# Fixing the order of high and low matmuls in the last gate tiles and in the output projection of a hybrid diffusion layer

## The chip, the cores and the metric

The kernel runs on one core of a Trainium2 chip. Its time is the device time of one launch in microseconds (us), taken without a profiler; the profile is one further execution. Each time below is from the runs of the kernel before, from its profile, or worked out from them as told.

## The reference

One transformer layer over 256 latent tokens and 256 context tokens of width 2048, in float32. Cut to the stages that this text speaks of:

```python
h_l = modulate(rms_norm(x, norm1_w), sh1, sc1)
# ... gated linear attention -> ya, differential attention -> yb
g_a, g_b = jnp.split(jax.nn.sigmoid(h @ w_gate + b_gate), 2, axis=-1)
mix = (g_a * (ya @ w_proj_gla) + g_b * (yb @ w_proj_diff)) @ w_out
x_new = x + g1 * mix
h2_l = modulate(rms_norm(x_new, norm2_w), sh2, sc2)
x_new = x_new + g2 * conv_ffn(h2_l, w_up, conv_w, conv_b, w_down)
```

`w_gate` is 2048 x 4096, `w_out` 2048 x 2048, `w_up` 2048 x 11264, `w_down` 5632 x 2048. A conditioning vector, multiplied by `w_ada`, gives the shifts, scales and gates (`sh1` to `g2`).

## The kernel before

**Halves.** TensorE works on float32 data that ScalarE and VectorE split in two: a rounded high half and the low half that is left. An activation block `A[k]` (128 channels by 256 tokens) holds both halves side by side, low first. A weight block of 512 columns (four 128 x 128 matrices, called a quad here) comes in by DMA as `wraw`; ScalarE copies it to `whi` (L206), and VectorE subtracts that to get `wlo` (L213); each of the two has four buffers in turn. For each 128 x 128 matrix there is a pair of matmuls: the high one (L262) multiplies `whi` with both halves of `A[k]`, 512 columns; the low one (L264) multiplies `wlo` with the high half of `A[k]`, 256 columns. A tile of 128 outputs is 16 pairs, or four quads, written by `col_tile`.

**Orders of a quad.** `col_tile` has three written orders: `TURN` is h0 l0 h1 l1 h2 l2 h3 l3 (h: high, l: low); `ENDED` ends in l2 l3 h3; `SHIFTED` is h0 h1 l0 h2 l1 h3 l2 l3, which draws the high halves one step ahead. Without a list of orders a tile has `TURN` three times and then `ENDED`, and this order only says in which order the program is written: a scheduler that simulates time while it builds places each engine's instructions, and it may take the high half of the next quad, or a matmul of another tile, ahead of a low half. With a list the tile is tied: each of its matmuls is held behind the one before it in the list, in one chain through all tied tiles (`chain`).

**Stages.** They follow one another on TensorE: a sweep over the first projections, the two attentions, 32 gate tiles (`gate_tile`, the last of them after the attention has ended), the two branch projections (`pga`, `pgb`), 16 output projection tiles (`mix`), six up tiles that are worked in an inner loop over k on activations that are not yet normalized (`up`, L1178 to L1180, inputs `raw0` to `raw15`), 82 up tiles by `col_tile` (`upg`, `upv`), and 16 down tiles of 11 quads each (`down`). The up tiles and the down tiles are tied already; their list puts `SHIFTED` at quads 0, 4, 7, 11, ... of nine (three for down) tiles and `ENDED` at the last of these.

**Between output projection and up tiles.** Each output projection tile is added to `x` (L1144, L1145), squared (L1150) and, from the ninth on, scaled to `raw` for the six unnormalized up tiles (L1124, L1125). The second sum of squares (`ss`, L1158) is a matmul of TensorE; from it ScalarE and VectorE make the root, and then normalize the 16 blocks one by one: `h2t` (L1166, VectorE), high half (L1167, ScalarE), low half (L1168, VectorE). The last of these blocks, k = 15, is called `a_1450` in the rows, the one before `a_1380`. Each engine works its queue strictly in the order in which the scheduler left it. The first upg tile reads block k with its k-th pair, so that its 16th pair needs `a_1450` whole.

```python
TURN = "h0 l0 h1 l1 h2 l2 h3 l3".split()
ENDED = "h0 l0 h1 l1 h2 l2 l3 h3".split()
SHIFTED = "h0 h1 l0 h2 l1 h3 l2 l3".split()
```

Of the kernel before, what the change touches and what calls it, by code (L numbers as in the profile page):

```python
# [146 lines left out]
def layer_kernel(tc, I, out):  # L147
# [3 lines left out]
    with es:  # L151
# [26 lines left out]
        def after(later, earlier):  # L178

            tc.add_manual_dep(later.ins, earlier.ins.name,  # L180
                              mybir.DependencyInfo(mybir.DependencyClass.NoSync, mybir.DependencyReason.DATA),
                              reason="activation table order")
# [14 lines left out]
        def flush(work=later):  # L197
            for step in [work.pop(0) for _ in range(len(work))]:
                step()

        def split(raw, n, lows=None):


            hi = st.tile([P, 512], F32R, tag="hi", bufs=4, name="whi")
            lo = st.tile([P, 512], F32R, tag="lo", bufs=4, name="wlo")
            copied[0] = S.copy(hi[:, :n], raw)  # L206
            if pin[0]:
                tc.keep_in_program_order(copied[0])
            splits[0] += 1
            e = G if splits[1] and splits[0] % splits[1] == 0 else V  # L210

            def low():
                i = e.tensor_tensor(lo[:, :n], raw, hi[:, :n].bitcast(F32), op=ALU.subtract)  # L213
                if pin[0]:
                    tc.keep_in_program_order(i)
                if e is V:
                    copied[1] = i

            if lows is None:
                low()  # L220
            else:
                lows.append(low)
            return hi, lo

        def fetch(src, n):
            raw = st.tile([P, 1024], F32, tag="raw", bufs=4, name="wraw")
            nc.sync.dma_start(raw[:, :n], src)
            return raw
# [5 lines left out]
        TURN = "h0 l0 h1 l1 h2 l2 h3 l3".split()  # L234
        ENDED = "h0 l0 h1 l1 h2 l2 l3 h3".split()
        SHIFTED = "h0 h1 l0 h2 l1 h3 l2 l3".split()

        def col_tile(src, acts, b, orders=None):

            nk = src.shape[1]
            nq = nk // 4
            tied = orders is not None
            orders = orders or [TURN] * (nq - 1) + [ENDED]
            for k0 in range(0, nk, 8):
                kn = min(8, nk - k0)
                if k0:  # L250
                    flush()
                raw = fetch(src[:, k0:k0 + kn, :].rearrange("p a b -> p (a b)"), kn * P)
                for kk in range(0, kn, 4):
                    whi, wlo = split(raw[:, kk * P:(kk + 4) * P], 4 * P)
                    order = orders[(k0 + kk) // 4]
                    for which in order:
                        j = int(which[1])
                        k = k0 + kk + j
                        sl = slice(j * P, (j + 1) * P)
                        first, last = k == 0 and which == "h0", k >= nk - 4 and which == order[-1]  # L260
                        if which[0] == "h":
                            i = PE.matmul(b.rearrange("p (a b) -> p a b", a=2), whi[:, sl], acts[k], start=first, stop=last)  # L262
                        else:
                            i = PE.matmul(b[:, T:], wlo[:, sl], acts[k][:, 1, :], start=False, stop=last)  # L264
                        if tied:
                            if chain:
                                after(i, chain[0])
                            chain[:] = [i]
                    if k0 and not kk:
                        flush(latest)  # L270
# [32 lines left out]
        A, B, C = [], [], []  # L303
# [350 lines left out]
        def ada_next(n):  # L654

            ada_due[0] += n
            while ada_at[0] < min(128, int(ada_due[0])):
                if len(ada_raw) == ada_pool[1]:
                    ada_dot()
                ada_load()  # L660
# [273 lines left out]
        with tc.tile_pool(name="diff", bufs=1) as pd:  # L934
# [96 lines left out]
            gates, ya, yb = {}, {}, {}  # L1031

            def gate_tile(j):
                ada_next(GATE_ADA[len(gates)])
                b = acc_bank("gate")
                col_tile(I["w_gate"][j], A, b)
                if j == len(C):
                    C.append(hp.tile([P, 2, T], F32, tag=f"c{j}", name=f"C{j}"))
                gates[j] = C[j % KT][:, j // KT, :]
                S.activation(gates[j], b[:, :T], AF.Identity, bias=vcol("b_gate", j))  # L1040
                V.tensor_tensor(gates[j], b[:, T:], gates[j], op=ALU.add)
# [6 lines left out]
            order = [j for k in range(KT) for j in (k, KT + k)]  # L1048
# [41 lines left out]
        for c in range(KT):  # L1090
# [7 lines left out]
            for b, j in ((ba, c), (bb, 16 + c)):  # L1098
                t = p3.tile([P, T], F32, tag="pt", bufs=2, name="pt")
                i = added(t, b)  # L1100
# [29 lines left out]
        for c in range(KT):  # L1130
            b = acc_bank("mix")
            if 0 < c < half:
                ada_next(1)
            col_tile(I["w_out"][c], A, b)
            if c == half:
                ada_done(16)
                ada_done(32)
                V.tensor_scalar(a2, adav[:, 32:48], 1.0, None, op0=ALU.add)
                V.tensor_tensor(a2, a2, vcol("norm2", 0, 16), op=ALU.mult)
                V.tensor_scalar(a2, a2, -0.5 / D, None, op0=ALU.mult)  # L1140
            xr = p3.tile([P, T], F32, tag="xr", bufs=2, name="xr")
            nc.scalar.dma_start(xr, I["xl"][:, c, :])
            x1.append(C[c][:, 0, :])
            V.scalar_tensor_tensor(xr, b[:, :T], adav[:, c:c + 1], xr, op0=ALU.mult, op1=ALU.add)  # L1144
            i = V.scalar_tensor_tensor(x1[c], b[:, T:], adav[:, c:c + 1], xr, op0=ALU.mult, op1=ALU.add)  # L1145
            if c >= half:
                for k in range(2 * (c - half), 2 * (c - half) + 2):
                    unnormed(k, i, summed)
            sq = p3.tile([P, T], F32, tag="sq2" if c else "sq_sum", bufs=2 if c else 1, name="sq2")
            S.activation(sq, x1[c], AF.Square)  # L1150
            if c == 0:
                sq_sum = sq
            elif c < KT - 1:
                summed = G.tensor_tensor(sq_sum, sq_sum, sq, op=ALU.add)
# [43 lines left out]
        with tc.tile_pool(name="ffn", bufs=1) as pf:  # L1198
# [25 lines left out]
                split_act(g[:, 1, :], g[:, 0, :], ug)  # L1224
                gs.append(g)

            def orders(n, nq, first, last):


                shifted = [i for j in range(0, nq * (last - first + 1) - 3, 7) for i in (first * nq + j, first * nq + j + 4)]  # L1230
                q = range(n * nq, (n + 1) * nq)
                return [ENDED if i == (last + 1) * nq - 1 else SHIFTED if i in shifted else TURN for i in q]

            for j in range(UPS // 2):
                gated(j, ups[2 * j], ups[2 * j + 1])
            for j in range(UPS // 2, FT):
# [11 lines left out]
            for c in range(KT):  # L1248
                b = acc_bank("down")
# [21 lines left out]
```

## Time and profile before

| what | us |
|---|---|
| time, median of three runs | 1700.16 |
| lowest, highest | 1699.24, 1700.27 |
| time of the profiled execution | 1700.9 |
| its span, first to last instruction | 1699.1 |
| TensorE busy in the span | 1680.0 |

The profiled execution took 0.7 us more than the median, and 1.8 us of its time lie outside the span. The granted clock is a mean of 0.999 of full speed. A matmul's duration covers its pipeline, so that neighbours overlap: what a matmul costs is the distance from its start to the next start, and not its duration.

### The profile page before, as it was taken

What the parts mean: (1) busy time and instruction counts of PE and PEld (TensorE: products, weight loads), DVE (VectorE), ACT (ScalarE), POOL (GpSimd) and SP (SyncE); (2) the same over time, 40 slices, a digit from 0 to 9 for tenths busy, and PEclk for the clock granted to TensorE, in tenths of its full rate; (3) what the DMA queues carried; (4) which work ended last, traced back from release to release, by engine and by line L of the source; (5) the groups of instructions that cost most, each with busy time, mean ns of one, the idle gap of its engine ahead of it and who ended that gap; (6) DMA issues with size and microseconds to landing.
All of it is one profiled execution on the core that took longest, in us unless ns stands there. A gap on an engine that the chain in (4) does not pass through costs nothing.

```text
span 1699.1 us, 29122 instructions
## 1 busy us (share of the span) xinstructions
PE 1680.0 (99%) x10460; PEld 1461.7 (86%) x10460; DVE 1241.0 (73%) x2375; ACT 980.0 (58%) x1984; POOL 310.9 (18%) x331
## 2 busy tenths in 40 slices
PE   7999999999999999999999999999999999999999
PEld 5779999998787888888888998888888888888887
DVE  5556765867688888788988797787878787644443
ACT  5324554756355777666766686666666666444443
POOL 0000213131210000001323200222222222222222
PEclk9999999999999999999999999999999999999999
DMA  9995532434566555688777566676767676666664
GB/s 384 402 408 194 165 127 90 140 109 155 181 200 233 172 188 186 203 280 279 267 260 261 181 200 217 217 238 224 237 227 237 222 241 223 199 203 193 199 201 135
DMA packets 108451, 368.75 MB, mean 217 GB/s; under 512 B 12176, under 2 KB 17040, under 8 KB 108304
## 3 DMA queue, kind: packets, MB, share of 16 engines
q1 hardware_dynamic: 103264, 362.51, 64.0%
q10 hardware_dynamic: 5040, 4.37, 0.8%
q8 instruction: 82, 1.34, 0.3%
q14 instruction: 65, 0.53, 0.1%
HBM read 364.73 MB, written 2.10 MB: 216 GB/s over the span
## 4 chain that ended last, share of the span: by engine, by line
PE 91%; DMA 4%; DVE 3%; ACT 1%; issue 1%; POOL 0%; SPq 0%; DVEq 0%; ACTq 0%
PE down L262 9%; PE upg L262 9%; PE upv L262 9%; PE gate L262 7%; PE down L264 5%; PE upg L264 5%; PE sweep L350 5%; PE upv L264 4%; PE gate L264 4%; PE mix L262 4%; PE mix L264 2%; PE pgb L262 2%; PE ab L350 2%; PE pga L262 2%; DMA ada<-in_w_ad 2%; PE dk L313 2%
## 5 line engine op out<-in xcount | busy, mean ns | idle before, releaser
L206 ACT CAST whi<-wraw 128x512 fp32r<-128x512 f32 (+2 forms) x1004 | 606.5, 608 | 397.3 <-PE down L262 110.5
L213 DVE TENSOR_TENSOR wlo<-wraw,whi 128x512 fp32r<-128x512 f32 (+2 forms) x888 | 608.6, 694 | 251.9 <-ACT whi L206 242.1
L213 POOL TENSOR_TENSOR wlo<-wraw,whi 128x512 fp32r<-128x512 f32 x116 | 157.0, 1353 | 576.4 <-ACT whi L206 555.5
L262 PE MATMUL down<-g,whi 128*128 128x512 f32 x704 | 243.6, 392 | 0.0
L262 PE MATMUL upg<-a,whi 128*128 128x512 f32 x656 | 229.0, 391 | 0.0
L262 PE MATMUL upv<-a,whi 128*128 128x512 f32 x656 | 229.0, 391 | 0.0
L264 PE MATMUL down<-g,wlo 128*128 128x256 f32 x704 | 195.4, 280 | 0.7 <-DVE wlo L213 0.7
L264 PE MATMUL upv<-a,wlo 128*128 128x256 f32 x656 | 182.8, 280 | 0.0
L264 PE MATMUL upg<-a,wlo 128*128 128x256 f32 x656 | 182.6, 280 | 0.0
L262 PE MATMUL gate<-a,whi 128*128 128x512 f32 x512 | 180.5, 398 | 0.7 <-ACT whi L206 0.7
L338 DVE CUSTOM_DVE_ANT_0 araw<-araw,cb 128x1024 f32<-128x1024 f32 x128 | 159.5, 1248 | 11.4 <-DMA araw<-in_w_ada 11.3
L262 PEld LDWEIGHTS down<-g,whi 128*128 128x128 f32 x704 | 131.0, 187 | 28.3
L262 PEld LDWEIGHTS upv<-a,whi 128*128 128x128 f32 x656 | 122.4, 187 | 26.6
L262 PEld LDWEIGHTS upg<-a,whi 128*128 128x128 f32 x656 | 122.4, 187 | 26.5
L264 PE MATMUL gate<-a,wlo 128*128 128x256 f32 x512 | 140.4, 284 | 0.0
L264 PEld LDWEIGHTS down<-g,wlo 128*128 128x128 f32 x704 | 132.9, 189 | 1.9 <-DVE wlo L213 1.0
L264 PEld LDWEIGHTS upv<-a,wlo 128*128 128x128 f32 x656 | 123.9, 189 | 0.5
L264 PEld LDWEIGHTS upg<-a,wlo 128*128 128x128 f32 x656 | 123.9, 189 | 0.5
L262 PEld LDWEIGHTS gate<-a,whi 128*128 128x128 f32 x512 | 94.4, 188 | 20.5 <-ACT whi L206 1.0
L264 PEld LDWEIGHTS gate<-a,wlo 128*128 128x128 f32 x512 | 96.5, 189 | 6.2 <-issue 1.8
L262 PE MATMUL mix<-a,whi 128*128 128x512 f32 x256 | 88.8, 396 | 0.0
L264 PE MATMUL mix<-a,wlo 128*128 128x256 f32 x256 | 69.0, 280 | 0.0
(343 smaller groups left out, 3324.9 us busy)
## 6 DMA issues: line engine op xcount, KB each, us to landing
wraw<-in_w_up SPq DMA_DIRECT2D x164, 512.0 KB, 4.3
araw<-in_w_ada SPq DMA_DIRECT2D x128, 512.0 KB, 4.9
wraw<-in_w_down SPq DMA_DIRECT2D x80, 512.0 KB, 3.9
ada<-in_w_ad SPq DMA_DIRECT2D x64, 512.0 KB, 10.0
wraw<-in_w_gate SPq DMA_DIRECT2D x64, 512.0 KB, 4.3
wraw<-in_w_in SPq DMA_DIRECT2D x58, 512.0 KB, 4.2
wraw<-in_w_proj SPq DMA_DIRECT2D x32, 512.0 KB, 4.3
wraw<-in_w_out SPq DMA_DIRECT2D x32, 512.0 KB, 4.6
```

The lines of the kernel that those rows point to most:

```text
L206: copied[0] = S.copy(hi[:, :n], raw)
L213: i = e.tensor_tensor(lo[:, :n], raw, hi[:, :n].bitcast(F32), op=ALU.subtract)
L262: i = PE.matmul(b.rearrange("p (a b) -> p a b", a=2), whi[:, sl], acts[k], start=first, stop=last)
L264: i = PE.matmul(b[:, T:], wlo[:, sl], acts[k][:, 1, :], start=False, stop=last)
L313: PE.matmul(o, whi[:, sl], hi[k], start=first and j == 0, stop=False)
L338: i = V.tensor_tensor_reduce(raw, raw, cb[:, q * 1024:(q + 1) * 1024], 1.0, 0.0, op0=ALU.mult, op1=ALU.add, accum_out=ada2[:, j, q:q + 1])
L350: return kept(PE.matmul(*args, **kw))
```

## The change

The function that lists the orders moves out of the feed-forward stage to `col_tile`, and two more stages use it. `orders(n, nq, first, last)` gives the list for tile n of nq quads: `SHIFTED` at quads 0, 4, 7, 11, 14, 18, ... counted from tile `first`, `ENDED` at the last quad of tile `last`, `TURN` everywhere else. Gate tiles 24 to 31 get a list with `SHIFTED` in tiles 24 to 28; output projection tiles 3 to 15 get one with `SHIFTED` in tiles 3 to 8. What is computed, and the number of matmuls, stay the same.

```diff
+        def orders(n, nq, first, last):
+            shifted = [i for j in range(0, nq * (last - first + 1) - 3, 7) for i in (first * nq + j, first * nq + j + 4)]
+            q = range(n * nq, (n + 1) * nq)
+            return [ENDED if i == (last + 1) * nq - 1 else SHIFTED if i in shifted else TURN for i in q]
+
-        def col_tile(src, acts, b, orders=None):
+        def col_tile(src, acts, b, turns=None):
...
-            tied = orders is not None
-            orders = orders or [TURN] * (nq - 1) + [ENDED]
+            tied = turns is not None
+            turns = turns or [TURN] * (nq - 1) + [ENDED]
...
-                    order = orders[(k0 + kk) // 4]
+                    order = turns[(k0 + kk) // 4]
...
                 b = acc_bank("gate")
-                col_tile(I["w_gate"][j], A, b)
+                n = len(gates)
+                col_tile(I["w_gate"][j], A, b, orders(n, 4, 24, 28) if n > 23 else None)
...
-            col_tile(I["w_out"][c], A, b)
+            col_tile(I["w_out"][c], A, b, orders(c, 4, 3, 8) if c > 2 else None)
```

The queues of the two kernels as they are built show what the scheduler makes of this. In the changed kernel line numbers after 235 are 7 to 8 higher. GpSimd's and SyncE's queues stay as they were.

TensorE where gate tile 23 passes to tile 24, before (`a_219`, `a_330`, `a_402`, `a_481` are blocks 0 to 3, `a_1450` block 15):

```order
L264 MATMUL gate<-a_1450,wlo 128x256
L262 MATMUL gate<-a_1450,whi 128x512
L262 MATMUL gate<-a_219,whi 128x512
L264 MATMUL gate<-a_219,wlo 128x256
L262 MATMUL gate<-a_330,whi 128x512
L264 MATMUL gate<-a_330,wlo 128x256
L262 MATMUL gate<-a_402,whi 128x512
L264 MATMUL gate<-a_402,wlo 128x256
L262 MATMUL gate<-a_481,whi 128x512
L264 MATMUL gate<-a_481,wlo 128x256
```

The same place in the changed kernel:

```order
L271 MATMUL gate<-a_1450,wlo 128x256
L269 MATMUL gate<-a_1450,whi 128x512
L269 MATMUL gate<-a_219,whi 128x512
L269 MATMUL gate<-a_330,whi 128x512
L271 MATMUL gate<-a_219,wlo 128x256
L269 MATMUL gate<-a_402,whi 128x512
L271 MATMUL gate<-a_330,wlo 128x256
L269 MATMUL gate<-a_481,whi 128x512
L271 MATMUL gate<-a_402,wlo 128x256
L271 MATMUL gate<-a_481,wlo 128x256
```

The high half of block 1 moved ahead of the low half of block 0, and so on to the end of the quad.

TensorE in the six unnormalized up tiles, before, from the last use of the first `raw` block (`raw_10507`) by the tile `up_11012` to the second use of the third block (`raw_10577`) by that tile:

```order
L1179 MATMUL up_11012<-raw_10507,whi 128x258
L1180 MATMUL up_11012<-raw_10507,wlo 128x258
L1178 MATMUL up_11012<-raw_10512,whi 128x258
L1179 MATMUL up_11012<-raw_10512,whi 128x258
L1180 MATMUL up_11012<-raw_10512,wlo 128x258
L1179 MATMUL up_11011<-raw_10577,whi 128x258
L1180 MATMUL up_11011<-raw_10577,wlo 128x258
L1158 MATMUL ss_11043<-sq_11007,ones 128x256
L1178 MATMUL up_11012<-raw_10577,whi 128x258
L1179 MATMUL up_11012<-raw_10577,whi 128x258
```

The same in the changed kernel:

```order
L1187 MATMUL up_11012<-raw_10507,whi 128x258
L1188 MATMUL up_11012<-raw_10507,wlo 128x258
L1186 MATMUL up_11012<-raw_10512,whi 128x258
L1187 MATMUL up_11012<-raw_10512,whi 128x258
L1188 MATMUL up_11012<-raw_10512,wlo 128x258
L1186 MATMUL up_11012<-raw_10577,whi 128x258
L1187 MATMUL up_11012<-raw_10577,whi 128x258
```

The two matmuls on `up_11011` went earlier, and the second sum of squares (`ss`, row L1158 before) went nine matmuls later, so that only four matmuls are left between the last use of one high half and the first use of the one that takes its buffer.

ScalarE at the first upg tile, before: the copies are `whi` of that tile's four quads and of the next tile, `shift` and `C_...` belong to the six up tiles' convolutions:

```order
L206 CAST whi<-wraw 128x512 x3
L1190 COPY shift<-up_11009 128x1
L1190 COPY shift<-up_11010 128x1
L1190 COPY shift<-up_11011 128x1
L1167 ACTIVATE a_1380<-h2t,adav 128x256
L1190 COPY shift<-up_11012 128x1
L1190 COPY shift<-up_11013 128x1
L1190 COPY shift<-up_11014 128x1
L1167 ACTIVATE a_1450<-h2t,adav 128x256
L206 CAST whi<-wraw 128x512
```

The same in the changed kernel, from the high half of `a_1380` to that of `a_1450`:

```order
L1175 ACTIVATE a_1380<-h2t,adav 128x256
L206 CAST whi<-wraw 128x512
L1200 ACTIVATE C_8721<-C_8721,shift 128x256
L1200 ACTIVATE C_8604<-C_8604,shift 128x256
L1219 ACTIVATE C_6289<-C_8721,vec 128x256
L1200 ACTIVATE C_8487<-C_8487,shift 128x256
L206 CAST whi<-wraw 128x512
L1219 ACTIVATE C_6569<-C_8604,vec 128x256
L1200 ACTIVATE C_8370<-C_8370,shift 128x256
L1219 ACTIVATE C_6846<-C_8487,vec 128x256
L206 CAST whi<-wraw 128x512
L1175 ACTIVATE a_1450<-h2t,adav 128x256
```

Three copies for the next tile (its quads 0, 1 and 2) and seven convolution steps now stand ahead of `a_1450`; before it was the fourth instruction after `a_1380`.

VectorE at the same place, before:

```order
L1168 SCALAR_TENSOR_TENSOR a_1380<-h2t,adav,a_1380 128x256
L1191 TENSOR_TENSOR C_8370<-up_11012,n2y 128x256
L1191 TENSOR_TENSOR C_8253<-up_11013,n2y 128x256
L1191 TENSOR_TENSOR C_8074<-up_11014,n2y 128x256
L1168 SCALAR_TENSOR_TENSOR a_1450<-h2t,adav,a_1450 128x256
L213 TENSOR_TENSOR wlo<-wraw,whi 128x512
L1212 SCALAR_TENSOR_TENSOR C_6289<-C_8721,vec,C_6289 128x255
```

The same in the changed kernel:

```order
L1176 SCALAR_TENSOR_TENSOR a_1380<-h2t,adav,a_1380 128x256
L213 TENSOR_TENSOR wlo<-wraw,whi 128x512
L1220 SCALAR_TENSOR_TENSOR C_6289<-C_8721,vec,C_6289 128x255
L213 TENSOR_TENSOR wlo<-wraw,whi 128x512
L1220 SCALAR_TENSOR_TENSOR C_6569<-C_8604,vec,C_6569 128x255
L1220 SCALAR_TENSOR_TENSOR C_6846<-C_8487,vec,C_6846 128x255
L1222 SCALAR_TENSOR_TENSOR C_6289<-C_8721,vec,C_6289 128x255
L213 TENSOR_TENSOR wlo<-wraw,whi 128x512
L1176 SCALAR_TENSOR_TENSOR a_1450<-h2t,adav,a_1450 128x256
```

The low half of `a_1450` now stands behind three splits for the next tile and four convolution steps.

## Rows read from the trace of the kernel before

**Rows 1.** The page: busy time of the engines, and shares of the chain of work that ended last.
```profile
PE 1680.0 (99%) x10460; PEld 1461.7 (86%) x10460; DVE 1241.0 (73%) x2375; ACT 980.0 (58%) x1984; POOL 310.9 (18%) x331
...
PE 91%; DMA 4%; DVE 3%; ACT 1%; issue 1%; POOL 0%; SPq 0%; DVEq 0%; ACTq 0%
```

**Rows 2.** The chain of work that ended last, in order of time, in the gate stage: start, us, what. Each row is the two low halves that end a tile, l2 l3 of `ENDED`; of tiles 24 and 31.
```profile
739.95 0.24 PE gate L264 x2
...
779.52 0.24 PE gate L264 x2
```

**Rows 3.** The timeline of TensorE, tied up tiles in plain `TURN`: the first high half of tile 19 and of tile 81 (start, us, operation, tiles and shape, count).
```profile
1100.52 0.39 PE L262 MATMUL upv<-a,whi 128*128 128x512 f32 x1
...
1444.41 0.39 PE L262 MATMUL upv<-a,whi 128*128 128x512 f32 x1
```

**Rows 4.** The same view, tied up tiles with `SHIFTED`: the first high halves of tile 8 (two in a row, the first `SHIFTED` quad) and of tile 18.
```profile
1039.24 0.63 PE L262 MATMUL upg<-a,whi 128*128 128x512 f32 x2
...
1094.97 0.39 PE L262 MATMUL upg<-a,whi 128*128 128x512 f32 x1
```

**Rows 5.** The chain that ended last in the output projection: the two low halves in a row of tiles 2, 9, 10 and 14, and in tile 10 the one low half for which TensorE waited. In tiles 2 to 9 the two low halves are followed by the tile's last high half; in tiles 10 to 14 they are the tile's last matmuls.
```profile
885.79 0.24 PE mix L264 x2
...
925.36 0.24 PE mix L264 x2
...
928.89 0.30 PE mix L264
...
931.42 0.24 PE mix L264 x2
...
953.71 0.24 PE mix L264 x2
```

**Rows 6.** The timeline of TensorE at the first upg tile: its first high half, the high halves of blocks 14 and 15, and the first of the upv tile.
```profile
994.50 0.40 PE L262 MATMUL upg<-a,whi 128*128 128x512 f32 x1
...
999.72 0.39 PE L262 MATMUL upg<-a,whi 128*128 128x512 f32 x1
...
1000.07 0.39 PE L262 MATMUL upg<-a,whi 128*128 128x512 f32 x1
...
1000.41 0.39 PE L262 MATMUL upv<-a,whi 128*128 128x512 f32 x1
```

**Rows 7.** The timeline of ScalarE there; in brackets the engine's idle time before the row and what ended it.
```profile
995.57 0.56 ACT L1167 ACTIVATE a<-h2t,adav 128x256 fp32r<-128x256 f32 x1
996.38 0.62 ACT L206 CAST whi<-wraw 128x512 fp32r<-128x512 f32 x1 [0.26 <-ACT a L1167]
...
998.21 0.49 ACT L1192 ACTIVATE C<-C,shift 128x256 f32<-128x256 f32 x1
998.61 0.60 ACT L206 CAST whi<-wraw 128x512 fp32r<-128x512 f32 x1
999.12 1.09 ACT L1211 ACTIVATE C<-C,vec 128x256 f32<-128x256 f32 x2
1000.12 0.49 ACT L1192 ACTIVATE C<-C,shift 128x256 f32<-128x256 f32 x1
1000.52 0.60 ACT L206 CAST whi<-wraw 128x512 fp32r<-128x512 f32 x1
```

**Rows 8.** The timeline of VectorE there.
```profile
998.35 0.47 DVE L1168 SCALAR_TENSOR_TENSOR a<-h2t,adav,a 128x256 fp32r<-128x256 f32 x1
998.74 0.68 DVE L213 TENSOR_TENSOR wlo<-wraw,whi 128x512 fp32r<-128x512 f32 x1
999.35 0.48 DVE L1212 SCALAR_TENSOR_TENSOR C<-C,vec,C 128x255 f32<-128x255 f32 x1
999.74 0.68 DVE L213 TENSOR_TENSOR wlo<-wraw,whi 128x512 fp32r<-128x512 f32 x1
```

**Rows 9.** The timelines of TensorE and ScalarE in the six up tiles, around the second sum of squares.
```profile
964.33 0.28 PE L1179 MATMUL up<-raw,whi 128*128 128x258 f32 x1
964.46 0.28 PE L1180 MATMUL up<-raw,wlo 128*128 128x258 f32 x1
...
964.65 1.34 ACT L206 CAST whi<-wraw 128x384 fp32r<-128x384 f32 x3 [1.36 <-PE up L1179]
```

**Rows 10.** Two waits of TensorE in the timeline, and the busy times of stretches after the first of them: us, busy time and count of TensorE, weight loads, VectorE, ScalarE, GpSimd, granted clock, DMA share, GB/s.
```profile
463.38 0.50 PE L262 MATMUL dq<-a,whi 128*128 128x512 f32 x1 [1.51 <-DVE osq L288]
...
210.24 0.39 PE L313 MATMUL dk<-a,whi 128*128 128x256 f32 x1 [1.19 <-ACT gv L698]
...
464.00:467.40 3.40, 3.40 (x12) 2.81 (x12) 3.22 (x11) 1.59 (x3) 0.00 (x0) 0.50 0.02 5
467.40:471.00 3.60, 3.60 (x23) 3.18 (x22) 1.28 (x4) 0.91 (x3) 0.00 (x0) 1.00 0.13 39
```

**Rows 11.** The timeline of TensorE after two waits: a gr tile after one for a low half (the low half, then two high halves three pairs apart), and the dq tile of rows 10 once the clock was back (two high halves six pairs apart).
```profile
399.97 0.39 PE L264 MATMUL gr<-a,wlo 128*128 128x256 f32 x1 [0.42 <-DVE wlo L213]
...
401.60 0.40 PE L262 MATMUL gr<-a,whi 128*128 128x512 f32 x1
...
402.66 0.40 PE L262 MATMUL gr<-a,whi 128*128 128x512 f32 x1
...
467.83 0.39 PE L262 MATMUL dq<-a,whi 128*128 128x512 f32 x1
...
469.92 0.39 PE L262 MATMUL dq<-a,whi 128*128 128x512 f32 x1
```

More of the change, by code (lines that the diff above doesn't have):

```diff
@@ L1225, in gated @@
                 gs.append(g)
[L1227 to L1232, printed above, removed]
             for j in range(UPS // 2):
```

## The prediction

> **What bounds the kernel now.** I read the page first: TensorE is busy in 1680.0 of 1699.1 us, and 91% of the chain that ended last lies on it [rows 1]. A matmul's duration overlaps its neighbours', so busy time can't show whether TensorE goes at its best pace. For that I went to the chain and the timeline and took distances between starts, tile by tile; a tile is 16 pairs everywhere. In the gate stage the two low halves that end a tile stand at 739.95 and, seven tiles later, at 779.52: 39.57 / 7 = 5.653 us a tile [rows 2]. The tied up tiles in plain turn go from 1100.52 to 1444.41 in 62 tiles: 343.89 / 62 = 5.547 us [rows 3]. Same matmuls, same columns, no wait in either, and the reader is to see a difference of 0.106 us a tile that belongs to the order alone. In the output projection tiles 3 to 9 take (925.36 - 885.79) / 7 = 5.653 us, tiles 11 to 14 (953.71 - 931.42) / 4 = 5.573 us [rows 5]. So TensorE has a slow and a fast pace: the slow one stands where every tile ends in l l h and begins with h, the fast one where low and high alternate without end. The view read last is the first upg tile, with the engines that feed it [rows 6 to 8]: there no wait stands now.
>
> **The order of the halves: what it gives.** `SHIFTED` is not free. From up tile 8 (1039.24) to tile 18 (1094.97) ten tiles take 55.73 us [rows 4], where ten plain ones take 55.47; in these lie ten shifted quads and one ended one, so a shifted quad costs 0.26 / 10 = 0.026 us.
> Gate tiles 24 to 31: 8 x 0.106 = 0.85 us come back, less 6 shifted quads x 0.026 = 0.16: gain 0.69 us.
> Output projection: tiles 3 to 9 give 7 x 0.106 = 0.74; tiles 11 to 14 give 4 x 0.026 = 0.10. Tile 10 takes 6.06 us between its rows, less 0.24 for the high half that tile 9 still had to do, so 5.82; of that some 0.18 is a wait for a low half (0.30 in the chain, where others take 0.12) [rows 5]. VectorE's queue there is not changed, so I let the wait stand and count 5.82 - 0.18 - 5.55 = 0.09. Less 0.16 for six shifted quads: gain 0.78 us.
> Together 1.47 us. The most is 1.65, if tile 10's wait goes too. The least is 1.25: in both stages the first shifted quad follows an ended one, so that three high halves stand in a row, which no row of before shows; if this leaves the slow pace until the next shifted quad, each stage loses up to four quads, 4 x 0.027 = 0.11. The whole gain is on the path, since TensorE waits for nothing else in these tiles.
> A rule that speaks against this: the Trainium skill, page "TensorE: Matmul & The Clock Gate", section "Back-to-back issue gap", gives the gap as columns / 2.4 + 2.5 ns, by which a pair is 216 + 109 ns and a tile an estimated 5.2 us in whatever order. The trace shows neither that pace nor one pace [rows 2, 3], so the measurement decides; by that rule the gain would be nothing, which is the third rival below.
>
> **What moves behind it.** The tie also changes what the scheduler does after the last output projection tile, and this is the larger part.
> First place: in the six unnormalized up tiles four matmuls are left between the last use of one high half and the first use of the half that takes its buffer. Before, ScalarE started such a copy at 964.65, just after the matmul that it waited for, which starts at 964.33 and takes 0.28; a copy takes some 0.5, a matmul starts each 0.12 [rows 9]. So the new half is there 0.28 + 0.04 + 0.51 + 0.04 = 0.87 us after that last use begins, and TensorE wants it after 5 x 0.12 = 0.60: a new wait of 0.3 us (from 0, if ScalarE comes earlier by something that I don't see, to 0.6).
> Second place: the first upg tile. Its 16th pair reads block 15 and starts at 1000.07 [rows 6]; block 15 was whole at 998.35 + 0.47 = 998.82 [rows 8], so 1.25 us early. In the changed kernel three copies of the next tile's high halves stand ahead of it on ScalarE, and these wait for their buffers, which the running tile holds. The first such copy starts at 996.38, when the tile's first quad has been read, and the next at 998.61 after four convolution steps; both hold as before, with the same steps between [rows 7]. Then, by the distances of the same rows: a step with `vec` until 999.12 + 0.50 = 999.62, one with `shift` until 1000.02, the second with `vec` ends at 1000.02 + 0.59 = 1000.61, the third copy starts at 1000.52, the high half of block 15 at 1001.03. VectorE's queue is worse: the convolution step on `C_6846` waits for 1000.61; then two steps of 0.39, the third split with 0.60, and block 15 with 0.47 [rows 8]: 1000.65 + 0.78 + 0.60 + 0.47 = 1002.50. With 0.05 to be seen by TensorE it goes on at 1002.55 and not at 1000.07: a wait of 2.5 us. TensorE takes its matmuls in order, so nothing fills it; all that stands behind (the upv tile, every tile after) comes 2.5 us later. Its ends: 0, if block 15 is not late after all, and 3.0, if VectorE, which gets the root later by the nine matmuls, is still half a us behind here. I take 2.5.
> What is late next: the upv tile's fourth quad, whose low half comes after some ten more steps of VectorE, at about 1006.3 by the same distances; it is wanted at 1002.55 + 0.35 + 12 x 0.347 = 1007.1. That is 0.8 us of cover, enough, but not much.
> Third: the clock. Before, TensorE idled 1.51 us ahead of 463.38, and from 464.0 to 467.4 the granted clock was 0.50 (1.2 instead of 2.4 GHz); after 1.19 us of idling at 210.24 it stayed at full speed [rows 10]. A wait of 2.5 us is longer than the one that was followed by a fall. The price is read from the same rows: 12 matmuls in 3.40 us, which at the pace after (23 in 3.60) take 1.88, so 1.5 us lost. Its ends are 0 and 1.5; I take 1.5.
>
> **The sum.** - 1.47 + 0.3 + 2.5 + 1.5 = + 2.8 us. On the profiled execution's 1700.9 that is 1703.7; that execution was 0.7 above the median of 1700.16, and against the median, which is what will be measured, it is **1703.0 us**.
>
> **Rivals.**
> *The clock holds.* The wait comes, but no fall follows; for it speaks that a wait of 1.19 us passed without one, and that TensorE is busy right up to this wait and right after it. 1700.16 - 1.47 + 2.8 = 1701.5 us.
> *No wait at block 15.* The queues of ScalarE and VectorE would have to run ahead of my distances by 2.5 us, or the tile to read later. Against it: both queues are strict and their waits were read one by one. 1700.16 - 1.47 + 0.3 = 1699.0 us.
> *The order buys nothing.* The pace would then belong to the place and not to the order, and the change wouldn't do what it says. Against it: within the output projection the pace changes at tile 10, where the order does [rows 5]. With the waits: 1700.16 + 4.3 = 1704.5 us.
> *The pace falls after the wait* (the case that ends clearly slower). Tied up tiles 0 to 7 are plain turn and keep whatever pace they start with. After a wait of 0.42 us the gr tile went on at 1.06 / 3 = 0.353 us a pair, the slow pace; after the longer one the dq tile went on at 2.09 / 6 = 0.348, the fast one [rows 11]. If TensorE comes out of the wait at block 15 in the slow pace, up tiles 1 to 7 cost 7 x 0.106 = 0.74 us more, until the first shifted quad in tile 8 ends it: 1703.0 + 0.7 = 1703.7 us, past the bound of 0.2%. It decides if tiles 1 to 7 take 5.65 us each.
> *The lateness goes on.* The upv tile's fourth quad uses up its 0.8 us of cover and TensorE waits again for about 1 us: 1704.0 us.
>
> **How the numbers follow.** Chances: the forecast 0.45 (1702.3 to 1703.8 by its own terms), the clock holds 0.20, the pace falls 0.13, no wait 0.12, the order buys nothing 0.06, the lateness goes on 0.04. The range goes from 1698.9 to 1704.6: its lower end takes in the case without a wait, which is the only one on the faster side, its upper end the order that buys nothing. A measurement of this kernel can tell about 0.2% (3.4 us) from no change, so slower begins at 1703.56 and faster ends at 1696.76. Slower: a quarter of the forecast's 0.45, three quarters of the pace's 0.13, and both last cases, 0.11 + 0.10 + 0.10 = 0.31, taken as 0.30. Faster: the gain is 1.65 us at most, so only an error of mine in kind, 0.03. Same: 0.67.
>
> **What would show it.** Gate tiles 29 to 31 at 5.547 us and tiles 24 to 28 near 5.58; output projection tiles 9 to 15 at 5.547 but for a wait of some 0.2 in tile 10; a wait of 0.3 us in the six up tiles ahead of a high half; in the first upg tile a wait of about 2.5 us for VectorE's low half of block 15, with the granted clock at 0.5 for some us behind it; all later tiles as before. I am wrong if block 15 is there in time (then the time is near 1699), if the two stages keep 5.653, or if the wait is longer than 3 us.

## The result and the profile after

The changed kernel takes 1704.41 us (median of 10, 1702.74 to 1704.97) where the kernel before takes 1699.87 us (10, 1698.20 to 1700.81): a ratio of 1.0027, interval [1.0017, 1.0037], 4.5 us slower. The prediction said + 2.8 us, 1703.0. Two more series gave 1704.37 beside 1700.01 (1.0026 [1.0015, 1.0037]) and 1704.51 beside 1699.56 (1.0030 [1.0018, 1.0042]). Each of the three series has one profile of the changed kernel; they are called I, II and III below. They differ, and that they do is half of the answer.

The page of profile I, the lines that answer to [rows 1], and the group of the first upg tile, whose idle time before it is new:

```profile
PE 1678.3 (99%) x10460; PEld 1460.2 (86%) x10460; DVE 1240.3 (73%) x2375; ACT 980.3 (58%) x1984; POOL 306.5 (18%) x331
...
PE 92%; DVE 4%; DMA 2%; ACT 1%; issue 1%; ACTq 0%; DVEq 0%
...
L269 PE MATMUL upg<-a,whi 128*128 128x512 f32 x656 | 229.6, 392 | 2.5 <-DVE a L1176 2.5
```

The page says little: TensorE is 99% busy in both. One thing stands out, the wait of 2.5 us for VectorE's line 1176, which makes the low half of a block. The rest needs starts, tile by tile.

The gate tiles, timeline of TensorE in profile I: the first high half of tile 25, the first high half of the first projection tile (behind tile 31), the last high half ahead of the new wait, and that projection tile's first low half.

```profile
738.69 0.63 PE L269 MATMUL gate<-a,whi 128*128 128x512 f32 x2
...
777.66 0.39 PE L269 MATMUL pga<-ya,whi 128*128 128x512 f32 x1
777.89 0.40 PE L269 MATMUL pgb<-yb,whi 128*128 128x512 f32 x1
778.50 0.39 PE L271 MATMUL pga<-ya,wlo 128*128 128x256 f32 x1 [0.20 <-DVE wlo L213]
```

(777.66 - 738.69) / 7 = 5.567 us a tile, where [rows 2] have 5.653. The last row is a new wait: the low half starts 0.61 us after the high half before it, where 0.23 is usual. In profile III this distance is 1.29 us:

```profile
779.49 0.40 PE L269 MATMUL pgb<-yb,whi 128*128 128x512 f32 x1
780.78 0.39 PE L271 MATMUL pga<-ya,wlo 128*128 128x256 f32 x1 [0.90 <-DVE wlo L213]
```

VectorE in profile I shows what it waits for: a transfer of the streamed ada weights, whose product stands ahead of that low half in its queue.

```profile
776.60 1.23 DVE L345 CUSTOM_DVE_ANT_0 araw<-araw,cb 128x1024 f32<-128x1024 f32 x1 [1.58 <-DMA araw<-in_w_ada]
777.75 0.08 DVE L345 DVE_READ_ACCUMULATOR2_ANT ada<- 128x1 f32 x1
777.75 1.89 DVE L213 TENSOR_TENSOR wlo<-wraw,whi 128x512 fp32r<-128x512 f32 x3
```

The output projection, profile I: first high halves of tiles 4 and 10, in tile 10 the late low half and the high half before it, and the first high halves of tiles 11 and 15.

```profile
890.00 0.63 PE L269 MATMUL mix<-a,whi 128*128 128x512 f32 x2
...
923.43 0.39 PE L269 MATMUL mix<-a,whi 128*128 128x512 f32 x1
...
926.20 0.39 PE L269 MATMUL mix<-a,whi 128*128 128x512 f32 x1
926.76 0.38 PE L271 MATMUL mix<-a,wlo 128*128 128x256 f32 x1 [0.17 <-DVE wlo L213]
...
929.42 0.39 PE L269 MATMUL mix<-a,whi 128*128 128x512 f32 x1
...
951.61 0.39 PE L269 MATMUL mix<-a,whi 128*128 128x512 f32 x1
```

Tiles 4 to 9 take 33.43 / 6 = 5.572 us, tile 10 takes 5.99, tiles 11 to 14 take 22.19 / 4 = 5.547. The same two tile starts in profile II:

```profile
930.19 0.40 PE L269 MATMUL mix<-a,whi 128*128 128x512 f32 x1
...
952.82 0.40 PE L269 MATMUL mix<-a,whi 128*128 128x512 f32 x1
```

22.63 / 4 = 5.657 us a tile: the same program and the same plain turn, now in the slow pace. That is the first surprise.

Block 15, profile I. TensorE, then ScalarE, then VectorE; these answer to [rows 6 to 8].

```profile
997.88 0.28 PE L271 MATMUL upg<-a,wlo 128*128 128x256 f32 x1
1000.63 0.50 PE L269 MATMUL upg<-a,whi 128*128 128x512 f32 x1 [2.47 <-DVE a L1176]
```
```profile
998.38 0.60 ACT L206 CAST whi<-wraw 128x512 fp32r<-128x512 f32 x1
998.88 0.50 ACT L1175 ACTIVATE a<-h2t,adav 128x256 fp32r<-128x256 f32 x1
```
```profile
998.31 0.88 DVE L1220 SCALAR_TENSOR_TENSOR C<-C,vec,C 128x255 f32<-128x255 f32 x2
999.10 0.48 DVE L1222 SCALAR_TENSOR_TENSOR C<-C,vec,C 128x255 f32<-128x255 f32 x1
999.49 0.69 DVE L213 TENSOR_TENSOR wlo<-wraw,whi 128x512 fp32r<-128x512 f32 x1
1000.09 0.48 DVE L1176 SCALAR_TENSOR_TENSOR a<-h2t,adav,a 128x256 fp32r<-128x256 f32 x1
```

The wait stands where the forecast put it: VectorE comes to the low half of block 15 behind the splits and convolution steps that now precede it and ends it at 1000.57. TensorE goes on 2.75 us after its last start, where 0.12 is usual, so 2.64 us are lost (the starts to the nanosecond give 2.752 and 0.117).

Behind the wait, first high halves of up tiles 2 and 8 in profile I:

```profile
1006.74 0.40 PE L269 MATMUL upg<-a,whi 128*128 128x512 f32 x1
...
1040.66 0.63 PE L269 MATMUL upg<-a,whi 128*128 128x512 f32 x2
```

33.92 / 6 = 5.653: the slow pace. And the clock, profile II: the wait, and the windows behind it (columns as in [rows 10]).

```profile
1001.91 0.51 PE L269 MATMUL upg<-a,whi 128*128 128x512 f32 x1 [2.47 <-DVE a L1176]
```
```profile
1002.28:1005.69 3.41, 3.41 (x13) 2.92 (x12) 3.41 (x9) 3.02 (x9) 0.00 (x0) 0.50 0.11 43
1005.69:1009.10 3.41, 3.41 (x21) 2.97 (x21) 3.41 (x9) 2.63 (x6) 0.00 (x0) 1.00 0.44 156
```

In profile II the granted clock falls to 1.2 GHz for 3.41 us behind the wait; in profile I the same stretch stays at full speed:

```profile
1001.00:1004.41 3.41, 3.41 (x21) 2.99 (x20) 3.41 (x9) 3.02 (x9) 0.00 (x0) 1.00 0.09 31
```

The differences of the three profiles against before, from the starts of the same matmuls (distance after less distance before, us):

| stretch | predicted | I | II | III |
|---|---|---|---|---|
| gate tiles 24 to 31 | -0.69 | -0.68 | -0.68 | -0.68 |
| the projection tiles behind them (wait for a low half) | 0 | +0.50 | +0.08 | +1.20 |
| output projection tiles 3 to 9 | -0.58 | -0.57 | -0.57 | -0.57 |
| tile 10 | -0.09 | +0.18 | +0.20 | +0.20 |
| tiles 11 to 14 | -0.10 | -0.11 | +0.33 | +0.32 |
| tile 15 and the six up tiles | +0.3 | +0.05 | +0.12 | +0.14 |
| first upg tile with its wait | +2.5 | +2.81 | +2.87 | +3.15 |
| up tile 1 | +1.5 (clock) | +0.10 | +1.50 | +1.23 |
| up tiles 2 to 17 | 0 | +0.74 | +0.01 | +0.65 |
| sum | +2.8 | +3.0 | +3.8 | +5.6 |

(The tie's predicted gain of 0.78 us in the output projection is cut into its three parts.) The mean of the three sums is + 4.2 us, near the measured 4.5. In these profiles other stretches differ too, without the change: the profile of before holds a fall of the clock at 464 us [rows 10], which I and II do not have and III has; it is left out of the sums.

### The profile page after: what moved, and what is told of

Read it like the earlier page. It is cut to its first block, busy times and chain, and to the rows that moved or that the text cites. A ratio compares the mean times of both kernels' runs of the same rounds, so it can differ in the third digit from the quotient of the medians.

```text
span 1701.0 us, 29131 instructions
## 1 busy us (share of the span) xinstructions
PE 1678.3 (99%) x10460; PEld 1460.2 (86%) x10460; DVE 1240.3 (73%) x2375; ACT 980.3 (58%) x1984; POOL 306.5 (18%) x331
## 4 chain that ended last, share of the span: by engine, by line
PE 92%; DVE 4%; DMA 2%; ACT 1%; issue 1%; ACTq 0%; DVEq 0%
PE down L269 9%; PE upg L269 9%; PE upv L269 9%; PE gate L269 7%; PE sweep L357 5%; PE down L271 5%; PE upg L271 4%; PE upv L271 4%; PE gate L271 4%; PE mix L269 3%; PE ab L357 2%; DMA araw<-in_w_ada 2%; PE pgb L269 2%; PE pga L269 2%; PE dk L320 2%; PE dk L322 2%
```

## The experiments

The theory under test: the loss comes from the output projection's tie alone, by what it moves behind itself; the wait at block 15 is its core, the clock and TensorE's pace behind it are its consequences. Each expectation below names its own theory A and rival B.

**One tie at a time.** First the gate tiles alone:

```diff
-            col_tile(I["w_out"][c], A, b, orders(c, 4, 3, 8) if c > 2 else None)
+            col_tile(I["w_out"][c], A, b)
```

> Only the eight gate tiles are tied; the output projection is as before. Theory A (the loss comes from the output projection's tie and what it moves behind itself): the gate tiles gain 0.68 us, the projection after them gives back 0.5 us of that in a new wait for its first low half, as the changed kernel's trace showed at 778; no wait at block 15, up tiles 0 to 7 at 5.547 us each; 1699.7 us against 1699.9 before. Rival B (the gate's tie is part of the loss, for what it moves in the queues): 1700.5 us or more.

Measured 1699.53 us, ratio 0.9999 [0.9990, 1.0008]. In its profile the gate tiles gain 0.68 us, and 0.48 of them are lost again ahead of the first projection low half. Then the output projection alone:

```diff
-                col_tile(I["w_gate"][j], A, b, orders(n, 4, 24, 28) if n > 23 else None)
+                col_tile(I["w_gate"][j], A, b)
```

> Only the output projection is tied, the gate tiles are as before. Theory A: the whole loss is here, the wait of 2.6 us at block 15 and up tiles 1 to 9 at the slow pace (about 0.84 us) as in the changed kernel: 1704.4 + 0.2 = 1704.6 us. Rival B (the loss is shared between the two ties): about 1702 us.

Measured 1703.39 us, ratio 1.0024 [1.0014, 1.0034], between the two theories' numbers (1704.6 and about 1702). But its profile has the whole wait, 2.75 us from start to start, and there is none in the profile with the gate tiles alone; so the loss is here. In this profile neither the clock nor the pace fell behind the wait (tiles 2 and 8):

```profile
1006.87 0.40 PE L269 MATMUL upg<-a,whi 128*128 128x512 f32 x1
...
1040.15 0.62 PE L269 MATMUL upg<-a,whi 128*128 128x512 f32 x2
```

33.28 / 6 = 5.547 us a tile.

**Block 15 first.** The next tile's copies and splits, and the convolution's first steps, are put behind block 15:

```diff
             copied[0] = S.copy(hi[:, :n], raw)
+            if held:
+                after(copied[0], held[0])
...
-            S.activation(u, u, AF.Identity, bias=shift[:, j:j + 1])
+            after(S.activation(u, u, AF.Identity, bias=shift[:, j:j + 1]), last[0])
...
+                held[:] = last if j == UPS // 2 else []
                 col_tile(I["w_up"][2 * j + 1 - UPS], A, bv, orders(2 * j + 1 - UPS, KT // 4, 8, 16))
+                held.clear()
```

> The changed kernel, with TensorE's order untouched, but the two halves of block 15 ahead of the next tile's copies and of the convolution steps on ScalarE and VectorE. Theory A: the wait of 2.6 us in the first upg tile goes. If the clock falls behind that wait in the timed runs, 1.5 us go with it: 1704.4 - 2.6 - 1.5 = 1700.3 us; if it does not, 1701.8 us. On the pace: if the slow pace of up tiles 1 to 7 comes from the wait (the rival of the prediction), these tiles return to 5.547 us and 0.8 us more go; if it comes from the order at the end of the output projection, they stay at 5.65 us.

Measured 1701.97 us, ratio 1.0015 [1.0006, 1.0024]: 2.4 us less than the changed kernel. The wait at block 15 is gone, but part of the lateness came back in the next two tiles, where TensorE now waits for low halves:

```profile
999.15 0.38 PE L275 MATMUL upv<-a,wlo 128*128 128x256 f32 x1 [0.22 <-DVE wlo L215]
...
1006.08 0.39 PE L275 MATMUL upg<-a,wlo 128*128 128x256 f32 x1 [0.85 <-DVE wlo L215]
```

From the first upg tile to up tile 10 this profile loses 2.2 us against before. One would like to conclude that both engines are behind there, so that whatever they do last is late. The run doesn't show that, because the edit itself makes idle time: ScalarE, with all the held copies and convolution steps behind block 15, idles 1.94 us until the block's input is there, and VectorE then idles 1.23 us for the first copy. ScalarE, then VectorE:

```profile
995.75 0.51 ACT L1179 ACTIVATE a<-h2t,adav 128x256 fp32r<-128x256 f32 x1 [1.94 <-DVE h2t L1178]
```
```profile
998.40 0.69 DVE L215 TENSOR_TENSOR wlo<-wraw,whi 128x512 fp32r<-128x512 f32 x1 [1.23 <-ACT whi L206]
```

How much of the 2.2 us comes from this idle time stays open. Nor does the run decide about the pace, since new waits lie in the tiles that were to tell.

**The changed kernel again.**

> The changed kernel itself once more, for a second profile and more times. If the granted clock falls behind the wait at block 15 (the prediction), the profile shows a stretch of some 3.4 us at 0.50 after 1000 us and the time is near 1704.4; if it never falls there, a time above 1704 goes with falls elsewhere, as the one of before at 464 us, and the distance to before is 3.0 us from the tiles alone.

Measured 1704.37 us; the profile is II above: the fall stands behind the wait and costs 1.50 us in up tile 1, as the forecast had it.

**The output projection's last tile untied.**

```diff
-            col_tile(I["w_out"][c], A, b, orders(c, 4, 3, 8) if c > 2 else None)
+            col_tile(I["w_out"][c], A, b, orders(c, 4, 3, 8) if 2 < c < KT - 1 else None)
```

> The changed kernel, but the output projection's last tile (15) is not tied. By the queue orders everything behind the output projection then stands as in the kernel before. Theory A (the loss is what the tie of that last tile moves behind itself): no wait at block 15 and no fall of the clock behind it, up tiles 0 to 7 at 5.547 us. Gate tiles -0.68 us, the wait ahead of the first projection tile +0.1 to +0.5, output projection tiles 3 to 10 -0.57 + 0.2; tiles 11 to 14 gain 0.1 us if TensorE leaves tile 10's wait in the fast pace and lose 0.3 if in the slow one: 1698.9 to 1699.7 us against 1700.0, 1699.3 taken. Rival B (tied tiles as such make the queues late): the wait stays, 1703 us or more.

Measured 1700.00 us, ratio 1.0001 [0.9993, 1.0010]. Behind the output projection the tiles of its profile stand at the distances of before, within 0.02 us, and there is no wait at block 15. So the loss hangs on the last tile's tie, not on the twelve tiles before it. Nor is there a gain, where the expectation had 0.7 us: in the profile 0.76 us are given back ahead of the first projection low half, and tile 10 and the tiles behind it cost 0.5 more. TensorE left tile 10's wait in the slow pace here; first high halves of tiles 12 and 14:

```profile
935.59 0.40 PE L269 MATMUL mix<-a,whi 128*128 128x512 f32 x1
...
946.89 0.40 PE L269 MATMUL mix<-a,whi 128*128 128x512 f32 x1
```

11.30 / 2 = 5.65. **With one shifted quad behind that wait:**

```diff
-            col_tile(I["w_out"][c], A, b, orders(c, 4, 3, 8) if 2 < c < KT - 1 else None)
+            col_tile(I["w_out"][c], A, b, ([SHIFTED] + [TURN] * 3 if c == 11 else orders(c, 4, 3, 8)) if 2 < c < KT - 1 else None)
```

> As the kernel with tile 15 untied, with the first quad of output projection tile 11 shifted. Theory A (a plain turn keeps the pace in which TensorE left its last wait, and a shifted quad brings the fast one back): tiles 12 to 14 take 5.547 us each in every profile, whatever tile 10's wait left; 0 to 0.3 us less than without it, 1699.1 us. Rival B (the pace after a wait is not undone by a shifted quad): tiles 12 to 14 at 5.65 us where tile 10 leaves the slow pace.

Measured 1699.06 us, ratio 0.9998 [0.9989, 1.0007]. Tile 10 ends in the slow pace in this profile as well, and behind the shifted quad the same two starts are

```profile
934.32 0.40 PE L269 MATMUL mix<-a,whi 128*128 128x512 f32 x1
...
945.41 0.40 PE L269 MATMUL mix<-a,whi 128*128 128x512 f32 x1
```

11.09 / 2 = 5.545: the quad brings the fast pace back. The times don't tell the two kernels apart: their intervals overlap.

**The wait alone.** Into the kernel before, with nothing newly tied, only the late block 15 is put:

```diff
...
                     whi, wlo = split(raw[:, kk * P:(kk + 4) * P], 4 * P)
+                    if held and k0 + kk == 8:
+                        after(held.pop(), copied[0])
...
```

(`held` contains ScalarE's half of block 15 while the first upv tile is issued, so that this half goes behind the third copy for that tile; in the shorter form the 8 is a 4, and it goes behind the second.)

> The kernel before, no tile newly tied and TensorE's order untouched; ScalarE's half of block 15 is made to stand behind the first three copies of the next tile's high halves. Theory A (this order alone makes the loss): a wait of about 2.5 us in the first upg tile, 1700.0 + 2.6 = 1702.6 us where the clock holds and the pace is fast, + 0.8 where TensorE leaves the wait in the slow pace, + 1.5 where the clock falls: between 1702.6 and 1704.1 us, 1703.4 taken. Rival B (the loss needs the tied tiles): within 1 us of before.

Measured 1703.36 us, ratio 1.0022 [1.0013, 1.0031]: the wait alone makes most of the loss. In its profile the wait is 2.46 us by the trace's count (2.47 in profile II), and the clock fell behind it:

```profile
1000.95:1004.36 3.41, 3.41 (x11) 2.93 (x12) 3.41 (x9) 3.26 (x10) 0.00 (x0) 0.50 0.07 23
```

> The same with block 15 behind two copies instead of three. By the queues its low half then comes some 0.8 us late. Theory A (a fall of the clock needs the longer wait): the granted clock holds, 1700.0 + 0.8 = 1700.8 us, and up tiles 1 to 7 may be slow (+ 0.7). Rival B (any wait there is followed by a fall): a stretch of 3.4 us at 0.50 behind it, 1702.3 us.

Measured 1700.60 us, ratio 1.0009 [1.0000, 1.0018]. In its profile the wait is short, as the row below shows, and the clock holds; but the next upg tile waits for a low half, and between up tiles 2 and 8 the profile loses 1.09 us, by that wait and by the slow pace behind it.

```profile
998.56 0.50 PE L264 MATMUL upg<-a,whi 128*128 128x512 f32 x1 [0.24 <-DVE a L1170]
```

**A version that might beat both.** Tile 15 untied and the shifted quad in tile 11, as in the version with the quad above, and besides the ada weights asked for one gate tile earlier:

```diff
-GATE_ADA = [0.25] * 4 + [0.5] * 16 + [1] * 12
+GATE_ADA = [0.25] * 4 + [0.5] * 14 + [1] * 13 + [0]
```

> The kernel with tile 15 untied and the shifted quad in tile 11, and besides the streamed ada weights of the gate stage are asked for one gate tile earlier from tile 18 on, with none in tile 31. Theory A (the gate tiles' gain is given back ahead of the first projection tile because VectorE waits there for an ada transfer): that wait (0.08 to 0.76 us so far) goes and the 0.68 us stay: 0.4 us less than without this edit, 1698.9 us where before is 1699.7. Rival B (the wait there is for the projection weights themselves, or moves into an earlier gate tile): no less, 1699.3 us.

Measured 1698.89 us beside 1699.56, ratio 0.9996 [0.9987, 1.0005]: not to be told from before by the times. In the profile the wait ahead of the first projection low half is gone (0.23 from start to start), and 0.64 of the gates' 0.68 us stay:

```profile
778.08 0.40 PE L269 MATMUL pgb<-yb,whi 128*128 128x512 f32 x1
778.31 0.28 PE L271 MATMUL pga<-ya,wlo 128*128 128x256 f32 x1
```

**The pace behind the wait.** The changed kernel, with the first quad of the tile behind the wait shifted, and beside it the changed kernel once more:

```diff
-                col_tile(I["w_up"][2 * j + 1 - UPS], A, bv, orders(2 * j + 1 - UPS, KT // 4, 8, 16))
+                col_tile(I["w_up"][2 * j + 1 - UPS], A, bv, [SHIFTED] + [TURN] * 3 if j == UPS // 2 else orders(2 * j + 1 - UPS, KT // 4, 8, 16))
```

> The changed kernel, with the first quad of the upv tile right behind the wait at block 15 shifted. Theory A (the slow pace in up tiles 1 to 9 is left over from that wait and a shifted quad ends it): the wait of 2.7 us stays, up tiles 2 to 7 take 5.547 us in every profile; the executions that were slow there lose 0.8 us, the median 0.3 us or so: 1704.0 us. Rival B (the slow pace is not what the median pays): no difference from the changed kernel in the same job, 1704.4 us.

> The changed kernel a third time, beside the kernel with the shifted quad behind the wait: 1704.4 us. A third profile of the stretch behind the wait: by the two so far it has the clock at 0.50 for 3.4 us (+ 1.5), or up tiles 1 to 9 in the slow pace (+ 0.8), or, as where the output projection alone was tied, neither.

Measured 1702.93 us (1.0022 [1.0013, 1.0030]) and 1704.51 us (1.0030 [1.0018, 1.0042]). The intervals overlap, so the medians don't show a gain. In the first kernel's profile up tiles 2 to 7 are at 5.547 us although the clock fell; in the second's, profile III, the clock fell and they are at 5.65. But TensorE left the wait in the first profile with the distances that it also had where the output projection alone was tied, and there the pace was fast without a shifted quad. So this pair is inconclusive; that a shifted quad ends the slow pace is shown in output projection tile 11. It shows once more in up tiles 8 and 9, which hold the first shifted quads of the up tiles: tiles 2 to 7 stand at 5.65 us in I and III, and from tile 10 on both profiles take the same time a tile as before.

## Why the prediction was right, and where its sum was short

The direction, the place and the mechanism were right: the order's gain is real, and the low half of block 15 costs more than it. The number was less so, and that it lies in the range owes something to luck: 1704.41 us is above the forecast's own 1702.3 to 1703.8, and below the range's end of 1704.6 only because that end was put there for the rival by which the order buys nothing, and this rival didn't happen. Point by point:

*The order.* Gate tiles -0.68 in every profile (predicted -0.69), output projection tiles 3 to 9 -0.57 (-0.58), so the price of a shifted quad and the two paces hold, and the rival by which the order buys nothing falls.

*"The whole gain is on the path, since TensorE waits for nothing else in these tiles."* This step failed, for what lies behind the tiles: the first projection low half waits for VectorE, and that for an ada transfer, so 0.08 to 1.20 us (mean 0.59) are given back. An engine that arrives 0.7 us earlier at something that is set by a transfer has gained less. The three profiles show the cause: VectorE idles 1.58, 1.14 and 2.27 us for that transfer in I, II and III, and what TensorE loses is each time 1.06 to 1.08 us less. In the run with the earlier ada weights VectorE doesn't wait for it, and 0.04 us are lost. The rows of II and III:

```profile
777.34 1.23 DVE L345 CUSTOM_DVE_ANT_0 araw<-araw,cb 128x1024 f32<-128x1024 f32 x1 [1.14 <-DMA araw<-in_w_ada]
```
```profile
778.89 1.23 DVE L345 CUSTOM_DVE_ANT_0 araw<-araw,cb 128x1024 f32<-128x1024 f32 x1 [2.27 <-DMA araw<-in_w_ada]
```

*"VectorE's queue there is not changed, so I let the wait stand."* In tile 10 the wait grew instead: from a high half to the late low half behind it 0.31 us passed before (928.49 to 928.80) and 0.56 pass now (926.20 to 926.76), where 0.23 is usual, and the tile takes 0.18 to 0.20 us more instead of 0.09 less. The chain of profile I shows why the queue's order doesn't settle it: ScalarE's steps on `raw` blocks come first, then the copy, then the split.

```profile
923.78 0.91 ACT raw L1132 x3
...
925.38 0.61 ACT whi L206
...
926.02 0.70 DVE wlo L213
...
926.76 0.38 PE mix L271
```

That the first of these steps is released by the end of tile 9, so that the low half comes no earlier when TensorE gets through tile 10 faster, fits this chain but was not tried by itself.

*Six up tiles.* No new wait: no distance between matmuls of these tiles is above 0.13 us but those at the sums of squares. The predicted 0.3 had a lower end of 0, for a ScalarE that comes earlier, and that is what happened: TensorE takes the high half in question at 963.01 (profile I) without a wait, and ScalarE's copy of 960.56 lies well ahead of that. So I had taken a later matmul for the one that releases the copy, as it seems; this was not tried by itself. The stretch, tile 15 included, costs 0.05 to 0.14 us.

*Block 15.* The term was 2.5; the wait is 2.64 in all three profiles, and with the slower restart and the slow pace that the tile begins with, the tile costs 2.81 to 3.15 us more than before (in profile III the fall of the clock begins in this tile). So the distances that the forecast added up on both queues hold. What I called next in line, the upv tile's fourth quad, was in time.

*The clock.* The price was exact: + 1.50 us in profile II against 1.5. The forecast made it a certainty within its case; six profiles have this wait (I, II, III, the output projection alone, the wait alone, the shifted quad behind it), and the clock fell in four of them. The premise was one draw, too. The wait of 1.51 us ahead of the dq tile, from which the forecast argued [rows 10], is in all 13 profiles, 1.89 to 1.90 us from start to start, and the clock fell behind it in three of them. In profile I it held:

```profile
462.80 0.50 PE L269 MATMUL dq<-a,whi 128*128 128x512 f32 x1 [1.51 <-DVE osq L295]
```
```profile
463.40:466.80 3.40, 3.40 (x22) 2.92 (x21) 3.22 (x11) 2.29 (x5) 0.00 (x0) 1.00 0.02 5
```

The timed runs agree: a mean granted clock below 1.000, which counts a fall anywhere in the run, was recorded in 17 of 23 runs of the changed kernel and in 16 of 81 of the kernel before.

*The pace falls after the wait.* This rival, with a chance of 0.13 and a price of 0.74 us, happened in two of three profiles (+ 0.84 in I with tile 1, + 0.65 in III). And the same thing happened at tile 10, which the forecast didn't consider: tiles 11 to 14 cost + 0.33 in II and + 0.32 in III instead of -0.10. It isn't the tie's doing: in the run with the gate tiles alone, whose output projection is that of before, these four tiles took 0.21 us more than in the profile of before. The step that failed is the sentence that the difference of pace "belongs to the order alone". The order decides how a pace begins and ends; a wait can set it anew, and plain turn then keeps whatever it has.

So of the 1.7 us by which the sum was short (measured 4.5, predicted 2.8), the means of the three profiles place 0.6 in the projection's wait, 0.6 in output projection tiles 10 to 14 and 0.5 in the pace of up tiles 2 to 17. On the other side, the six up tiles cost 0.2 less than predicted, and the first upg tile and up tile 1 together 3.9 instead of 4.0. That makes 1.4, since the mean of the three sums is 4.2; where the other 0.3 lies three profiles can't tell.

## What to carry to other kernels

An order that makes a stretch faster isn't done at the stretch's end: look at who is late behind it, and tie the last tile only if the schedule behind it stays as it was; here untying one tile of thirteen took the whole loss away. Where an engine's pace has two values, try the quad that restores the fast one behind each wait, not only at set distances: here the profiles show the pace restored, but the times show no gain from it. And one profile is one draw: where waits, clock and pace vary from one execution to the next, a second profile of the same kernel is worth as much as an experiment.

## What the runs showed of the hardware

- Plain turn has two steady paces, 5.547 and 5.653 us a tile, and the same program takes the one or the other behind the same wait. Profile I goes on behind tile 10's wait (0.56 us from start to start) in the fast one, II and III in the slow one behind the same 0.56; of the nine profiles with this tile tied, three went on fast and six slow, and no row shows what decides it. One shifted quad brings the fast pace back; no tied stretch in plain turn was seen to change its pace without a wait before it.
- The same wait, 2.62 to 2.64 us, was followed by a fall of the granted clock from 2.4 to 1.2 GHz in four profiles of six, each time for 3.41 us, and beginning between 0.1 us before TensorE's restart and 1.3 us behind it. The wait of 1.51 us ahead of the dq tile was followed by one in three profiles of 13. The wait counted at 0.24 us in the short form had none behind it in its one profile. The Trainium skill, page "TensorE: Matmul & The Clock Gate", section "What's actually happening", says that the hardware's look at TensorE's activity runs free of the kernel; that agrees with a fall that comes in some executions and not in others, and the rows show no more than that.
- At 1.2 GHz a pair takes 0.64 us (the first three high halves of the upv tile in profile II start at 1002.43, 1003.07 and 1003.71). At 2.4 GHz it takes more than half of that, which would be 0.32: 0.347 us in the one pace and 0.353 in the other.
